# First stage of a decoder layer: the weights of modulation tile 0 in quarters and their sums shared out anew between TensorE and VectorE, the first hT tile in two PSUM banks, one norm weight loaded later

## The chip, the core and the metric

The kernel runs on one core of a Trainium2 chip. A core has a tensor engine (PE; its weight loads have a row of their own, PEld), a vector engine (DVE), a scalar engine (ACT), a further engine for general work (POOL), and a queue for loads and stores (SP); ACT and POOL can issue loads too. Each engine works through its own list in order, and waits where an instruction needs what another engine or a load has not delivered. PE writes its results to PSUM banks of 128 partitions by 512 values in float32. The metric is the device time of one execution in microseconds (us), the median of a few runs; lower is better.

## What is computed

One layer of a decoder with two token mixers beside each other and a gated MLP, float32, sequence 512, width 1024. The change touches what stands at the beginning:

```python
cs = jax.nn.silu(c)                                   # c: (1, 1024)
mod = cs @ w_ada[l] + b_ada[l]                        # six vectors of 1024
shift1, scale1, gate1, shift2, scale2, gate2 = ...
h = _rmsnorm(x, norm1_g[l]) * (1.0 + scale1) + shift1
proj = h @ w_in[l]                                    # columns of the mixers and gates
...
out = _rmsnorm(out, subln_g) * (1.0 - lam_init)       # heads of the second mixer
```

`x` is 512 by 1024, `w_ada` 1024 by 6144. The rest (attention, merging, output projection, MLP with a causal convolution, final norm) is unchanged in both kernels.

## The kernel before

The first stage makes the first 768 columns of `proj` (query, key and value of the first mixer). The width is cut into KT = 8 tiles of 128 features. For tile k the stage needs:

- two vectors of 128, the scale and the shift of the modulation. They are sums over 1024 inputs of `w_ada`, times `cs`. The weights of tile k lie in `adaw[k]`, 128 partitions by (j, kk, 128): j = 0 the scale's half, j = 1 the shift's half, kk = 0 to 7 the blocks of inputs. Each half is 512 KB. Some blocks are summed on PE directly (a matmul of the block with `cs` broadcast, `direct` and `direct0`), the others are added up by DVE (`add_a0`, `ac_ops`) and then summed over partitions by one closing matmul with ones (`reduce_mod`; line 474 for tile 0);
- `mods[k]`, made from these sums by `finish_mod`;
- x normalised and transposed: PE transposes four blocks of 128 rows into a bank `xt` (`turn` for tile 0, line 432; `h_turn` for the others, line 378);
- `hT`, scale and shift applied to `xt`: ACT writes a rounded copy `hTh` and an exact one `hf` (`h_tile`, line 383), DVE the remainder `hTl` (`h_low`, line 391);
- the weights `w0[k]` (128 by 768), split into a rounded part `w0h` (ACT, lines 361 and 363) and a remainder `w0l` (DVE, lines 369 and 371).

Then `mm_k` (line 403) multiplies: six groups i of 128 columns, each in a bank of its own (`acc6`, a0 to a5), and three products p: `w0h` by `hTh`, `w0l` by `hTh`, `w0h` by `hTl`. One product of one group is one matmul of 512 columns. The order of PE, DVE and ACT in this stage is that in which the code is written (`manual_schedule`, line 259); SP's order too (line 243). Later parts are ordered by a scheduler.

At the start x comes in as four blocks of 128 rows. For each, ACT takes the sum of squares (`stat`, line 414), POOL and DVE form the root, and DVE or ACT scale the first 256 columns; the other columns are scaled by ACT later (`scale_x`). `keep_warm` (line 184) issues matmuls with ones into a5 whose result nobody reads; they fill PE until data are there. For tile 0, PE sums blocks 0 to 4 of both halves and DVE blocks 5 to 7. The two sums lie in the banks `pa0` and a4.

From tile 1 on, one turn of the loop (line 482) is, for PE: the products p = 0 and 1 of tile gi, the closing sums of tile gi + 1, its transposes, and product p = 2 of tile gi. DVE adds up the weights of the tile after. In turn 0 the closing sums of tile 1, each behind two direct sums, stand before the two matmuls of group 5.

SP's list is: c (as 8 rows `crow8`, line 166), the four blocks of x, `adaw[0]` in two halves, `w0[0]`, then `adaw[k]` and `w0[k]` by turns (the tiles 1 to 4 in quarters of 256 KB, the others in halves), four small loads (lines 251 to 256), and the weights of the next stage (line 567). ACT issues three small loads at the start: `b_ada`, `norm1_g` and `diff_subln_g`, all into `rows`, which one transpose turns into columns (`cols`, line 272).

Of the kernel before, what the change touches and what calls it, by code (L numbers as in the profile page):

```python
# [14 lines left out]
P = 128  # L15
D = 1024
# [44 lines left out]
def kernel(  # L61
# [44 lines left out]
    def tbank(name, shape=(P, S)):  # L106
        return bank("t", 2, list(shape), name)
# [55 lines left out]


    crow8 = cpool.tile([8, P], F32, name="crow8")
    nc.sync.dma_start(crow8, c.rearrange("o (a p) -> (o a) p", p=P))
# [13 lines left out]
    def keep_warm(n):  # L180
        while n:
            m = min(n, 4)
            o = acc6[5].rearrange("p (a n) -> p a n", a=4)
            nc.tensor.matmul(o[:, :m], ones, ones4[:, :m], start=True, stop=True)
            n -= m
# [38 lines left out]
    def load_ada(k):  # L224
        if k % 3 == 2:
            aw = big.tile([P, 2, KT, P], F32, tag="out" + "hl"[k // 3], name=f"adaw{k}")
        else:
            aw = pp.tile([P, 2, KT, P], F32, tag="adaw", bufs=2, name=f"adaw{k}")
        cut = 4 if 0 < k < 5 else KT
        for a in range(0, KT, cut):  # L230
            for j, base in ((0, D), (1, 0)):
                nc.sync.dma_start(
                    aw[:, j, a : a + cut],
                    wada[a * P : (a + cut) * P, base + k * P : base + (k + 1) * P].rearrange("(a p) n -> p a n", p=P),
                )
        adaw[k] = aw
# [6 lines left out]
    with tc.manual_schedule(engines={nc.sync.engine}):  # L243
        for t in range(NT):
            nc.sync.dma_start(xn[:, t], xd[t * P : (t + 1) * P, :])
# [10 lines left out]
        nc.sync.dma_start(crow[66:88, :], conv_b[0].rearrange("(a p) -> a p", p=P))  # L256
# [15 lines left out]
    nc.tensor.transpose(pc, rows, ident[:NR, :NR])  # L272
    cols = cpool.tile([P, NR], F32, name="cols")
    nc.vector.tensor_copy(cols, pc)
    bsh, bsc1, n1g, sublnc = cols[:, 0:8], cols[:, 8:16], cols[:, 16:24], cols[:, 24:25]
# [28 lines left out]
    def direct(pa, j, k, kks, start=True, stop=False):  # L304
        for kk in kks:
            nc.tensor.matmul(
                pa[:, j],
                adaw[k][:, j, kk],
                cs[:, kk : kk + 1].to_broadcast([P, P]),
                start=start and kk == kks[0],  # L310
                stop=stop and kk == kks[-1],
            )

    def early_mod(gi):
        pa = tbank(f"pa{gi}", (P, 2, P))
        direct(pa, 0, gi, (6, 7))
        return pa

    def reduce_mod(gi, early=None):
        pa = early or tbank(f"pa{gi}", (P, 2, P))  # L320
        for j in range(2):
            if early:
                if j:
                    direct(pa, 1, gi, (6, 7))
                nc.tensor.matmul(pa[:, j], ac[gi][0][:, j], ones, start=False, stop=True)
            else:
                nc.tensor.matmul(pa[:, j, 0:1], ac[gi][0][:, j], ones[:, 0:1], start=True, stop=True)
        return pa

    def finish_mod(k, pa):  # L330
        pa = pa if k == 0 else [pa[:, 0], pa[:, 1]]
        m = pp.tile([P, 16], F32, tag="mod", bufs=3, name=f"mod{k}")
        last = nc.vector.scalar_tensor_tensor(
            m[:, 0:1], pa[0][:, 0:1], bsc1[:, k : k + 1], n1g[:, k : k + 1], ALU.add, ALU.mult
        )
        if k:
            nc.scalar.activation(m[:, 1:2], pa[1][:, 0:1], AF.Identity, bias=bsh[:, k : k + 1])
        else:
            nc.vector.tensor_add(m[:, 1:2], pa[1][:, 0:1], bsh[:, k : k + 1])
        mods[k] = m  # L340
        return last

    def w0_views(k):
# [29 lines left out]
    hfs, pts = {}, {}  # L373

    def h_turn(k):
        pts[k] = tbank(f"xt{k}")
        for t in range(NT):
            nc.tensor.transpose(pts[k][:, t * P : (t + 1) * P], xn[:, t, k * P : (k + 1) * P], ident)

    def h_tile(k, between=None):  # L380
        hf = pp.tile([P, S], F32, tag="hf", bufs=2, name=f"hf{k}")
        for dst in (hTh[k], hf):
            nc.scalar.activation(dst, pts[k], AF.Identity, bias=mods[k][:, 1:2], scale=mods[k][:, 0:1])
# [11 lines left out]
    def mm_k(k, part, some=DONE):  # L395
        wh, wl = wts[k]
        last = k == KT - 1
        if part == (2 if last else 1):
            return
        for i in some:  # L400
            for p in (1, 2) if last and part else (0, 1) if part == 0 and not last else (part,):
                lhs, rhs = ((wh, hTh), (wl, hTh), (wh, hTl))[p]
                nc.tensor.matmul(
                    acc6[i], lhs[:, i * P : (i + 1) * P], rhs[k], start=k == 0 and p == 0, stop=last and p == 2
                )

    keep_warm(WARM)
    rst = pp.tile([P, NT], F32, name="rst")
# [17 lines left out]
    def scale_head(t):  # L426
        nc.scalar.activation(xn[:, t, :HEAD], xn[:, t, :HEAD], AF.Copy, scale=rst[:, t : t + 1])

    pts[0] = tbank("xt0")

    def turn(t):
        nc.tensor.transpose(pts[0][:, t * P : (t + 1) * P], xn[:, t, 0:P], ident)
# [6 lines left out]
    DIRECT = 5  # L439

    def add_a0(j, kks):
        for kk in kks:
            w, f = adaw[0][:, j, kk], cs[:, kk : kk + 1]
            if kk == DIRECT:
                nc.vector.tensor_scalar_mul(a0[j], w, f)
            else:
                nc.vector.scalar_tensor_tensor(a0[j], w, f, a0[j], ALU.mult, ALU.add)

    def direct0(j):
        for kk in range(DIRECT):  # L450
            nc.tensor.matmul(
                pa0[j], adaw[0][:, j, kk], cs[:, kk : kk + 1].to_broadcast([P, P]), start=kk == 0, stop=False
            )
# [12 lines left out]
    scale_x(0)  # L466
    scale_head(2)
    scale_head(3)
    scale_x(1)
    direct0(0)  # L470
    turn(2)
    direct0(1)
    for j in range(2):
        nc.tensor.matmul(pa0[j], a0[j], ones, start=False, stop=True)
    turn(3)
    finish_mod(0, pa0)
    split_hi(0, 0)
    keep_warm(2)
    h_tile(0, lambda: split_hi(0, 1))
    split_lo(0, 0)  # L480

    for gi in range(KT):
# [8 lines left out]
        else:  # L491
# [64 lines left out]
        nc.scalar.copy(va, pv.rearrange("p (t d) -> p t d", t=NT))  # L556


    pcv = tbank("pcv", (P, 88))
    nc.tensor.transpose(pcv, crow, ident[:88, :88])  # L560
# [1499 lines left out]
```

## Time and profile before

| | |
|---|---|
| median of 3 runs | 685.23 us (684.86 to 685.31) |
| span of the profiled execution, first to last instruction | 684.1 us |
| busy: PE, PEld, DVE, ACT, POOL | 675.3, 589.7, 564.2, 384.5, 98.5 us |
| first matmul of the projection | at 15.36 us |
| first matmul of the next stage | at 55.59 us |
| DMA in the slices of 17.1 us from the start | 304, 349, 296, 181 GB/s |

The profile is one execution. A row of its timeline gives the start and the duration in us, the engine, the line of the kernel, the operation, its output and inputs, and how many instructions are merged in the row; in brackets stands how long the engine had been idle before and what ended that. Names are those of the program without buffer numbers: `a` is any of the banks a0 to a5 (or DVE's sums of tile 0), `w` stands for `w0`. A float32 matmul appears as two passes, a weight load and a matmul each. The windows give busy times of each engine in stretches of the span; the waits say who waited for whom.

### The profile page before, as it was taken

How to read it: one execution, taken by the hardware profiler on the slowest of the kernel's cores; microseconds unless marked ns; L12 is line 12 of the kernel's file. 1: busy time of each engine (PE TensorE's matmuls, PEld its weight loads, DVE VectorE, ACT ScalarE, POOL GpSimd, SP SyncE). 2: the span in 40 equal slices, each digit the busy share in tenths (PEclk: the TensorE clock that was granted, in tenths of full speed). 3: DMA queues.
4: the chain of work that ended last, by engine and by line, in shares of the span. 5: the costliest groups of instructions: out<-in, count | busy, mean ns of one | idle time of the engine just before them, and what ended most of it. 6: DMA issues, size and time to landing. Idle time of an engine off the chain costs nothing. (4 is left out here: it accounts for less than half of the span.)

```text
span 684.1 us, 11125 instructions
## 1 busy us (share of the span) xinstructions
PE 675.3 (99%) x4141; PEld 589.7 (86%) x4141; DVE 564.2 (82%) x1075; ACT 384.5 (56%) x688; POOL 98.5 (14%) x119
## 2 busy tenths in 40 slices
PE   9999999999999999999999999999999999999995
PEld 5887887878888888888899999999999998888885
DVE  4999875988796756974589988888888999979997
ACT  6776774546543223324377665666555665656765
POOL 3000000011012012021030111112120003440300
PEclk9999999999999999999999999999999999999999
DMA  9995422565456885659555788777978647995903
GB/s 304 349 296 181 144 62 64 163 166 162 144 157 181 255 246 158 217 144 345 187 93 109 170 216 212 180 165 207 216 194 216 153 170 186 191 205 146 166 1 123
DMA packets 117142, 123.89 MB, mean 181 GB/s; under 512 B 5063, under 2 KB 94184, under 8 KB 117088
## 3 DMA queue, kind: packets, MB, share of 16 engines
q1 hardware_dynamic: 97246, 95.11, 43.3%
q0 software_dynamic: 19648, 27.79, 24.1%
q8 instruction: 32, 0.52, 0.3%
q10 hardware_dynamic: 194, 0.28, 0.1%
q14 instruction: 22, 0.18, 0.1%
HBM read 118.97 MB, written 2.11 MB: 177 GB/s over the span
## 5 line engine op out<-in xcount | busy, mean ns | idle before, releaser
L1362 PE MATMUL up<-t,m_whi 128*128 128x256 f32 x512 | 93.1, 283 | 0.0
L1362 PEld LDWEIGHTS up<-t,m_whi 128*128 128x128 f32 x512 | 79.9, 192 | 0.0
L1362 PE MATMUL up<-t,m_wlo 128*128 128x256 f32 x256 | 72.4, 283 | 0.0
L1362 PE MATMUL up<-bh,p_whi 128*128 128x256 f32 x232 | 65.7, 283 | 0.0
L1362 PE MATMUL up<-bl,p_whi 128*128 128x256 f32 x232 | 65.7, 283 | 0.0
L1362 PE MATMUL up<-bh,p_wlo 128*128 128x256 f32 x232 | 65.7, 283 | 0.0
L952 POOL DMA_DIRECT2D arow<-arow x28 | 22.5, 804 | 247.8 <-DVE sd L821 123.6
L1362 PEld LDWEIGHTS up<-t,m_wlo 128*128 128x128 f32 x256 | 49.2, 192 | 0.0
L1271 POOL DMA_DIRECT2D s<-in_w_up_dram x21 | 26.9, 1353 | 141.3 <-DMA s<-in_w_up_dram 69.2
L1362 PEld LDWEIGHTS up<-bh,p_whi 128*128 128x128 f32 x232 | 44.5, 192 | 0.0
L1362 PEld LDWEIGHTS up<-bl,p_whi 128*128 128x128 f32 x232 | 44.5, 192 | 0.0
L1362 PEld LDWEIGHTS up<-bh,p_wlo 128*128 128x128 f32 x232 | 44.5, 192 | 0.0
L944 DVE SCALAR_TENSOR_TENSOR arow<-ra,cs,arow 128x512 f32<-128x512 f32 x56 | 41.8, 748 | 0.6
L1299 ACT CAST m_whi<-s 128x1024 fp32r<-128x1024 f32 x31 | 32.4, 1046 | 11.1 <-DVE s L1293 6.3
L1303 DVE TENSOR_TENSOR m_wlo<-s,m_whi 128x1024 fp32r<-128x1024 f32 x31 | 37.8, 1218 | 0.0
L1362 PE MATMUL up<-t,p_whi 128*128 128x256 f32 x176 | 32.2, 283 | 0.0
L1362 PEld LDWEIGHTS up<-t,p_whi 128*128 128x128 f32 x176 | 27.5, 192 | 0.0
L816 ACT ACTIVATE sd<-sd,dmx 128x128 f32<-128x128 f32 (+3 forms) x32 | 17.7, 557 | 17.3 <-DVE dmx L806 17.3
L1369 ACT ACTIVATE gT<-a,cv 128x512 f32<-128x512 f32 x22 | 17.7, 813 | 16.9 <-DVE a L1404 15.8
L1299 ACT CAST p_whi<-wa 128x1024 fp32r<-128x1024 f32 x18 | 18.7, 1041 | 12.6 <-PE up L1362 12.6
L1303 DVE TENSOR_TENSOR p_wlo<-wa,p_whi 128x1024 fp32r<-128x1024 f32 x18 | 22.0, 1222 | 3.8 <-ACT p_whi L1299 3.8
L1362 PE MATMUL up<-t,p_wlo 128*128 128x256 f32 x88 | 24.9, 283 | 0.0
(499 smaller groups left out, 2052.4 us busy)
## 6 DMA issues: line engine op xcount, KB each, us to landing
ra<-in_w_ada_dram SPq DMA_DIRECT2D x32, 512.0 KB, 4.9
wa<-in_w_up_dram SPq DMA_DIRECT2D x22, 512.0 KB, 4.2
s<-in_w_up_dram SPq DMA_DIRECT2D x21, 512.0 KB, 4.7
s<-in_w_up_dram POOLq DMA_DIRECT2D x21, 512.0 KB, 6.9
w<-in_w_in_dram SPq DMA_DIRECT2D x12, 512.0 KB, 5.0
a<-in_w_up_dram SPq DMA_DIRECT2D x11, 512.0 KB, 4.7
b<-in_w_down_dram SPq DMA_DIRECT2D x10, 512.0 KB, 4.2
adaw<-in_w_ada_dram SPq DMA_DIRECT2D x8, 512.0 KB, 6.3
```

The costliest lines, as they stand in the source:

```text
L816: exp = nc.scalar.activation(pm[m], pm[m], AF.Exp, bias=mx[:, m : m + 1], scale=slope, accum_out=ls)
L944: nc.vector.scalar_tensor_tensor(ac, r[:, a], cc, ac, ALU.mult, ALU.add)
L952: nc.gpsimd.dma_start(whole[0:n], whole[n : 2 * n], accum_op=ALU.add)
L1271: nc.gpsimd.dma_start(dst, upblock(*blk), accum_op=ALU.add)
L1299: nc.scalar.copy(W[J, name][0], R[J, SRC[name]])
L1303: nc.vector.tensor_sub(lo, R[J, SRC[name]], hi.bitcast(F32))
L1362: nc.tensor.matmul(o[u], w[:, k, cu], b[:, k], start=name in ("p1", "m5", "p2") and k == 0 and x == 0, stop=k == 3 and x == 2, skip_group_ ...
L1369: nc.scalar.activation(grow(j), av[J][:, u], AF.Identity, bias=cv[:, 66 + j : 67 + j], scale=cv[:, 44 + j : 45 + j])
```

## The change

Five edits, all but one of them to the first stage.

1. The load of c moves from SP's queue to ACT's, ahead of ACT's other two. `diff_subln_g` leaves `rows`; it is loaded by SP behind the convolution's bias into a row more of `crow`, and its column comes out of the later transpose of `crow` (`cv`).
2. `adaw[0]` is loaded in quarters, the two of the scale first.
3. The sums of tile 0 are shared out anew. Scale: blocks 0 to 5 on PE, 6 and 7 on DVE. Shift: blocks 0 and 1 on DVE, 2 to 7 on PE. Blocks are summed in the order in which they come, between the turns of x. The scale's part of `mods[0]` (`mod_scale`) is followed by the shift's. Two fillers go, and tile 1's transposes stand before `h_tile(0)`.
4. `xt` of tile 0 lies in two banks: rows 0 to 255 in a bank of its own, rows 256 to 511 in a5. `h_tile(0)` makes the first half of `hTh` on DVE and the second on ACT; `hf` in two pieces on ACT.
5. `mm_k` of tile 0 does all `w0h` products before the `w0l` products. Tile 1's four direct sums come together, then the two matmuls of group 5, then the two closing sums. The large part of tile 1's `w0l` is split behind `finish_mod`, as in the other turns.

```diff
-    nc.sync.dma_start(crow8, c.rearrange("o (a p) -> (o a) p", p=P))
-    NR = 16 + 8 + 1
+    nc.scalar.dma_start(crow8, c.rearrange("o (a p) -> (o a) p", p=P))
+    NR = 16 + 8
...
-    nc.scalar.dma_start(rows[24:25, :], diff_subln_g)
-    crow = cpool.tile([88, P], F32, name="crow")
+    crow = cpool.tile([89, P], F32, name="crow")
...
-        cut = 4 if 0 < k < 5 else KT
-        for a in range(0, KT, cut):
-            for j, base in ((0, D), (1, 0)):
+        cut = 4 if k < 5 else KT
+        pieces = [(a, j) for a in range(0, KT, cut) for j in range(2)]
+        if k == 0:
+            pieces.sort(key=lambda e: e[1])
+        for a, j in pieces:
+            for base in ((D, 0)[j],):
...
         nc.sync.dma_start(crow[66:88, :], conv_b[0].rearrange("(a p) -> a p", p=P))
+        nc.sync.dma_start(crow[88:89, :], diff_subln_g)
...
-    nc.vector.tensor_scalar_mul(sublnc, sublnc, -0.5 * (1.0 - LAM_INIT))
...
     def early_mod(gi):
         pa = tbank(f"pa{gi}", (P, 2, P))
-        direct(pa, 0, gi, (6, 7))
+        for j in range(2):
+            direct(pa, j, gi, (6, 7), start=j == 0)
         return pa
...
             if early:
-                if j:
-                    direct(pa, 1, gi, (6, 7))
-                nc.tensor.matmul(pa[:, j], ac[gi][0][:, j], ones, start=False, stop=True)
+                nc.tensor.matmul(pa[:, j], ac[gi][0][:, j], ones, start=False, stop=True, skip_group_check=True)
...
         for dst in (hTh[k], hf):
-            nc.scalar.activation(dst, pts[k], AF.Identity, bias=mods[k][:, 1:2], scale=mods[k][:, 0:1])
+            for src in pts[k]:
+                q = slice(src[1], src[1] + src[0].shape[-1])
+                if k == 0 and dst is not hf and src[1] == 0:
+                    nc.vector.tensor_scalar(dst[:, q], src[0], mods[k][:, 0:1], mods[k][:, 1:2], ALU.mult, ALU.add)
+                else:
+                    nc.scalar.activation(
+                        dst[:, q], src[0], AF.Identity, bias=mods[k][:, 1:2], scale=mods[k][:, 0:1]
+                    )
...
+        order = [(i, p) for i in some for p in ps_]
+        if k == 0:
+            order.sort(key=lambda e: e[1])
...
-    pts[0] = tbank("xt0")
+    HALF = S // 2
+    pts[0] = [(tbank("xt0", (P, HALF)), 0), (acc6[5][:, :HALF], HALF)]
...
-            keep_warm((4, 1)[t - 1])
+            if t == 1:
+                keep_warm(4)
+                direct0(0, range(4), True)
     root(2)
-    add_a0(0, range(DIRECT, DIRECT + 2))
+    add_a0(0, (6,), 6)
     root(3)
-    add_a0(0, range(DIRECT + 2, KT))
-    add_a0(1, range(DIRECT, KT))
+    add_a0(0, (7,), 6)
+    add_a0(1, (0, 1), 0)
     scale_x(0)
     scale_head(2)
     scale_head(3)
     scale_x(1)
-    direct0(0)
+    direct0(0, (4, 5))
+    direct0(1, (2, 3), True)
     turn(2)
-    direct0(1)
-    for j in range(2):
-        nc.tensor.matmul(pa0[j], a0[j], ones, start=False, stop=True)
+    sum0(0)
     turn(3)
-    finish_mod(0, pa0)
+    direct0(1, range(4, KT))
+    sum0(1)
+    mod_scale(0, pa0[0][:, 0:1])
+    nc.vector.tensor_add(mods[0][:, 1:2], pa0[1][:, 0:1], bsh[:, 0:1])
     split_hi(0, 0)
-    keep_warm(2)
+    h_turn(1)
     h_tile(0, lambda: split_hi(0, 1))
     split_lo(0, 0)
...
-        if gi == 0:
-            h_turn(1)
         mm_k(gi, 0, DONE if gi else FIRST[:5])
         mm_k(gi, 1)
         if more:
+            early = None
             if gi == 0:
-                split_lo(1, 0)
-            pa = reduce_mod(gi + 1, early_mod(1) if gi == 0 else None)
-            if gi == 0:
+                early = early_mod(1)
                 mm_k(0, 0, FIRST[5:])
+            pa = reduce_mod(gi + 1, early)
...
             last_mod = finish_mod(gi + 1, pa)
-            if gi:
-                split_lo(gi + 1, 0)
+            split_lo(gi + 1, 0)
             split_lo(gi + 1, 1)
             h_tile(gi + 1)
...
-    nc.vector.tensor_copy(cv[:, :88], pcv)
+    nc.vector.tensor_copy(cv[:, :89], pcv)
+    sublnc = cv[:, 88:89]
+    nc.vector.tensor_scalar_mul(sublnc, sublnc, -0.5 * (1.0 - LAM_INIT))
```

The names in the rows below carry the program's numbers: `xt0` and `xt1` are the transposed tiles 0 and 1, `pa0` and `a4` the banks of tile 0's scale and shift, `a5` the bank of group 5 (and of the fillers), `a0_0` and `a0_1` DVE's sums of tile 0, `pa1` the bank of tile 1's sums. First PE's list at the start, behind the filler that follows turn 0, in the kernel before:

```order
L432 MATMUL xt0_205<-ident_69,xn_123 128x128
L184 MATMUL a5_113<-ones_67 128x128
L451 MATMUL pa0_206<-cs_188,adaw0_130 128x128 x5
L432 MATMUL xt0_205<-ident_69,xn_123 128x128
L451 MATMUL a4_111<-cs_188,adaw0_130 128x128 x5
L474 MATMUL pa0_206<-ones_67,a0_0_207 128x128
L474 MATMUL a4_111<-ones_67,a0_1_208 128x128
L432 MATMUL xt0_205<-ident_69,xn_123 128x128
L184 MATMUL a5_113<-ones_67 128x256
L378 MATMUL xt1_307<-ident_69,xn_123 128x128 x4
```

And the same place in the changed kernel:

```order
L460 MATMUL pa0_207<-cs_190,adaw0_129 128x128 x4
L442 MATMUL xt0_206<-ident_69,xn_122 128x128
L460 MATMUL pa0_207<-cs_190,adaw0_129 128x128 x2
L460 MATMUL a4_110<-cs_190,adaw0_129 128x128 x2
L442 MATMUL a5_112<-ident_69,xn_122 128x128
L466 MATMUL pa0_207<-ones_67,a0_0_208 128x128
L442 MATMUL a5_112<-ident_69,xn_122 128x128
L460 MATMUL a4_110<-cs_190,adaw0_129 128x128 x4
L466 MATMUL a4_110<-ones_67,a0_1_209 128x128
L377 MATMUL xt1_285<-ident_69,xn_122 128x128 x4
```

Ten direct sums have become twelve; four of them now stand behind the last turn instead of five, and the scale's closing sum has moved ahead of it. Next PE's list at the end of tile 0's `w0l` products, up to the first product with `hTl`, before:

```order
L403 MATMUL a4_111<-hThA_116,w0l0_283 128x512
L306 MATMUL pa1_323<-cs_188,adaw1_135 128x128 x2
L325 MATMUL pa1_323<-ones_67,ac1_0_289 128x128
L306 MATMUL pa1_323<-cs_188,adaw1_135 128x128 x2
L325 MATMUL pa1_323<-ones_67,ac1_0_289 128x128
L403 MATMUL a5_113<-hThA_116,w0h0_282 128x512
L403 MATMUL a5_113<-hThA_116,w0l0_283 128x512
L403 MATMUL a0_110<-hTlA_118,w0h0_282 128x512
```

And in the changed kernel:

```order
L412 MATMUL a4_110<-hThA_115,w0l0_283 128x512
L308 MATMUL pa1_323<-cs_190,adaw1_136 128x128 x4
L412 MATMUL a5_112<-hThA_115,w0h0_282 128x512
L412 MATMUL a5_112<-hThA_115,w0l0_283 128x512
L327 MATMUL pa1_323<-ones_67,ac1_0_294 128x128 x2
L412 MATMUL a0_109<-hTlA_117,w0h0_282 128x512
```

Both closing sums of tile 1 (`ac1`) now stand behind the two matmuls into a5. Last DVE's list at the same time: the end of tile 1's sums (`ac`), its `mod`, the split of its `w0l`, and the start of tile 2's sums, before:

```order
L301 TENSOR_TENSOR ac_0_289<-ac_0_289,ac_1_298 128x256
L391 TENSOR_TENSOR hTlA<-hf_286,hThA 128x512
L369 TENSOR_TENSOR w0l_295<-w_1_140,w0h_294 128x512
L333 SCALAR_TENSOR_TENSOR mod_332<-pa_323,cols 128x1
L371 TENSOR_TENSOR w0l_295<-w_1_140,w0h_294 128x256
L286 TENSOR_SCALAR ac_1_352<-adaw_142,cs 128x256
```

And in the changed kernel:

```order
L303 TENSOR_TENSOR ac_0_294<-ac_0_294,ac_1_304 128x256
L397 TENSOR_TENSOR hTlA<-hf_290,hThA 128x512
L334 SCALAR_TENSOR_TENSOR mod_332<-pa_323,cols 128x1
L367 TENSOR_TENSOR w0l_301<-w_1_141,w0h_300 128x512
L369 TENSOR_TENSOR w0l_301<-w_1_141,w0h_300 128x256
L288 TENSOR_SCALAR ac_1_353<-adaw_143,cs 128x256
```

The large split of tile 1's `w0l` has moved from ahead of the `mod` to behind it, between the `mod` and tile 2's sums.

More of the change, by code (lines that the diff above doesn't have):

```diff
@@ L328, in reduce_mod, with mod_scale @@
         return pa
+    def mod_scale(k, pa):
+        m = mods[k] = pp.tile([P, 16], F32, tag="mod", bufs=3, name=f"mod{k}")
+        return nc.vector.scalar_tensor_tensor(m[:, 0:1], pa, bsc1[:, k : k + 1], n1g[:, k : k + 1], ALU.add, ALU.mult)
     def finish_mod(k, pa):
[L331 to L340, printed above, removed]
+        last = mod_scale(k, pa[:, 0, 0:1])
+        nc.scalar.activation(mods[k][:, 1:2], pa[:, 1, 0:1], AF.Identity, bias=bsh[:, k : k + 1])
         return last
@@ L375, in h_turn @@
     def h_turn(k):
-        pts[k] = tbank(f"xt{k}")
+        xt = tbank(f"xt{k}")
+        pts[k] = [(xt, 0)]
         for t in range(NT):
-            nc.tensor.transpose(pts[k][:, t * P : (t + 1) * P], xn[:, t, k * P : (k + 1) * P], ident)
+            nc.tensor.transpose(xt[:, t * P : (t + 1) * P], xn[:, t, k * P : (k + 1) * P], ident)
     def h_tile(k, between=None):
@@ L399, in mm_k @@
             return
[L400 to L405, printed above, removed]
+        ps_ = (1, 2) if last and part else (0, 1) if part == 0 and not last else (part,)
+        order = [(i, p) for i in some for p in ps_]
+        if k == 0:
+            order.sort(key=lambda e: e[1])
+        for i, p in order:
+            lhs, rhs = ((wh, hTh), (wl, hTh), (wh, hTl))[p]
+            nc.tensor.matmul(
+                acc6[i], lhs[:, i * P : (i + 1) * P], rhs[k], start=k == 0 and p == 0, stop=last and p == 2
+            )
     keep_warm(WARM)
@@ L427, in scale_head @@
         nc.scalar.activation(xn[:, t, :HEAD], xn[:, t, :HEAD], AF.Copy, scale=rst[:, t : t + 1])
-    pts[0] = tbank("xt0")
+    HALF = S // 2
+    pts[0] = [(tbank("xt0", (P, HALF)), 0), (acc6[5][:, :HALF], HALF)]
     def turn(t):
-        nc.tensor.transpose(pts[0][:, t * P : (t + 1) * P], xn[:, t, 0:P], ident)
+        nc.tensor.transpose(pts[0][t // 2][0][:, t % 2 * P : (t % 2 + 1) * P], xn[:, t, 0:P], ident)
     def scale_x(t):
@@ L447, in add_a0, with direct0, sum0 @@
                 nc.vector.scalar_tensor_tensor(a0[j], w, f, a0[j], ALU.mult, ALU.add)
-    def direct0(j):
-        for kk in range(DIRECT):
+    def direct0(j, kks, start=False):
+        for kk in kks:
             nc.tensor.matmul(
-                pa0[j], adaw[0][:, j, kk], cs[:, kk : kk + 1].to_broadcast([P, P]), start=kk == 0, stop=False
-            )
+                pa0[j], adaw[0][:, j, kk], cs[:, kk : kk + 1].to_broadcast([P, P]), start=start and kk == kks[0],
+                stop=False,
+            )
+    def sum0(j):
+        nc.tensor.matmul(pa0[j], a0[j], ones, start=False, stop=True)
     for t in range(NT):
@@ L556, in turn_va @@
         nc.scalar.copy(va, pv.rearrange("p (t d) -> p t d", t=NT))
-    pcv = tbank("pcv", (P, 88))
-    nc.tensor.transpose(pcv, crow, ident[:88, :88])
+    pcv = tbank("pcv", (P, 89))
+    nc.tensor.transpose(pcv, crow, ident[:89, :89])
     cv = cpool.tile([P, P], F32, name="cv")
-    nc.vector.tensor_copy(cv[:, :88], pcv)
+    nc.vector.tensor_copy(cv[:, :89], pcv)
+    sublnc = cv[:, 88:89]
+    nc.vector.tensor_scalar_mul(sublnc, sublnc, -0.5 * (1.0 - LAM_INIT))
     def load_cols(src, col, name):
```

8 lines of the change are left out of this document (4 added, 4 removed).

## The prediction

> **What bounds the kernel now.** I read the page first (busy time per engine), then the busy time by stretches, then the timeline of the first 56 us, where every edit lies.
>
> ```profile
> span 684.1 us, 11125 instructions
> 100.00:200.00 100.00, 100.00 (x578) 80.29 (x577) 80.63 (x231) 53.66 (x129) 10.73 (x12) 1.00 0.46 132
> ```
>
> The first row is the page's span. The second is one stretch of the windows (us, then busy time and count of PE, PE's weight loads, DVE, ACT and POOL): from 100 to 200 us PE is busy for all 100.00 us, with DVE at 80.63. So PE sets the end, and an edit before 56 us is worth what it moves PE's last wait there, no more. The three timed runs (684.86 to 685.31, median 685.23) lie 0.8 to 1.2 us above this span; I carry that part over unchanged and make the sum against the span.
>
> **The start, up to the first matmul of the projection.** The columns are start, duration, engine, line, output and inputs, count, and in brackets the idle time before.
>
> ```profile
> 9.28 0.34 PE L432 MATMUL xt<-ident,xn 128*128 128x128 f32 x1
> 9.45 1.02 PE L184 MATMUL a<-ones 128*128 128x512 f32 x2
> 10.31 0.29 PE L432 MATMUL xt<-ident,xn 128*128 128x128 f32 x1
> 12.41 1.19 PEld L451 LDWEIGHTS a<-cs,adaw 128*128 128x128 f32 x10 [0.31 <-DMA adaw<-in_w_ada_dram]
> 13.52 0.30 PEld L474 LDWEIGHTS pa<-ones,a 128*128 128x128 f32 x2
> 13.85 0.39 PE L474 MATMUL a<-ones,a 128*128 128x128 f32 x2
> 14.28 0.16 DVE L339 TENSOR_TENSOR mod<-a,cols 128x1 f32<-128x1 f32 x1
> 14.53 0.78 ACT L383 ACTIVATE hThA<-xt,mod 128x512 fp32r<-128x512 f32 x1 [0.59 <-DVE mod L339]
> 15.36 0.50 PE L403 MATMUL a<-hThA,w0h 128*128 128x512 f32 x1
> 15.70 0.39 PE L403 MATMUL a<-hThA,w0l 128*128 128x512 f32 x1
> ```
>
> Ten weight loads of the direct sums fill 12.41 to 13.52, 0.111 us a pass. They wait for the shift half of tile 0's weights (0.31 us, DMA). The last sum's two passes start at 13.85; DVE adds at 14.28 (0.43 later), ACT starts the first hT at 14.53 (0.25 later), and PE's first projection matmul starts at 15.36, 0.05 after ACT's 0.78 us.
>
> In the new order PE's list from 9.28 is: turn 0; one filler of two 512-column passes, 9.45 to 10.31; four direct sums (8 passes, to 11.20), turn 1 (11.31), two direct sums of the scale (11.75), two of the shift (12.20), turn 2 (12.31), the scale's closing sum (12.53), turn 3 (12.64), four direct sums of the shift (13.53), its closing sum at 13.53. That is 0.32 earlier than 13.85. Do its inputs come in time?
>
> ```profile
> 11.90 0.35 DVE L447 SCALAR_TENSOR_TENSOR a<-adaw,cs,a 128x128 f32<-128x128 f32 x1
> 12.08 0.51 ACT L427 ACTIVATE xn<-xn,rst 128x256 f32<-128x256 f32 x1 [0.31 <-DVE rst L205]
> 8.37 0.35 DVE L424 TENSOR_SCALAR xn<-xn,rst 128x256 f32<-128x256 f32 x1
> 11.27 0.49 ACT L427 ACTIVATE xn<-xn,rst 128x256 f32<-128x256 f32 x1
> ```
>
> DVE's last piece of the scale ends at 12.25 and ACT's scaling for turn 3 at 12.59, both before they are needed; the shift's last quarter is needed at 12.64 and landed by 12.41. So PE's own list binds here, and data that come sooner don't help. DVE adds at 13.96, ACT starts at 14.21. ACT now does 256 columns: not under 0.49 (the last row, 256 columns from SBUF) nor over 0.78; I take 0.55, near the row of its size. DVE's half (0.35 in the third row, 256 columns from SBUF; at most 0.78) starts at 14.15 and is covered by ACT's half unless it takes over 0.6. First matmul at 14.8 instead of 15.36: **0.55 us gained** (0.3 to 0.6). The low half of the weights, which DVE makes after its hT half (at about 14.5 to 15.2), is wanted only after five high matmuls (at about 15.9), so that delay is hidden by the new order of tile 0.
>
> **Tile 1: the gain is spent.** The next rows are the sum of tile 1, the DVE work around it, and the same points of tiles 2 and 3.
>
> ```profile
> 18.34 0.69 DVE L369 TENSOR_TENSOR w0l<-w,w0h 128x512 fp32r<-128x512 f32 x1
> 18.88 0.39 PE L325 MATMUL pa<-ones,ac 128*128 128x128 f32 x2
> 19.30 0.22 DVE L333 SCALAR_TENSOR_TENSOR mod<-pa,cols 128x1 f32<-128x1 f32 x1 [0.28 <-PE pa L325]
> 19.44 0.41 DVE L371 TENSOR_TENSOR w0l<-w,w0h 128x256 fp32r<-128x256 f32 x1
> 19.77 0.35 DVE L286 TENSOR_SCALAR ac<-adaw,cs 128x256 f32<-128x256 f32 x1
> 19.85 0.78 ACT L383 ACTIVATE hThA<-xt,mod 128x512 fp32r<-128x512 f32 x1
> 20.94 0.40 PE L403 MATMUL a<-hThA,w0h 128*128 128x512 f32 x1
> 22.90 0.42 DVE L301 TENSOR_TENSOR ac<-ac,ac 128x256 f32<-128x256 f32 x1
> 23.73 0.50 PE L327 MATMUL pa<-ones,ac 128*128 128x1 f32 x4
> 24.09 0.63 PE L378 MATMUL xt<-ident,xn 128*128 128x128 f32 x4
> 28.68 0.61 PE L327 MATMUL pa<-ones,ac 128*128 128x1 f32 x4
> 29.15 0.63 PE L378 MATMUL xt<-ident,xn 128*128 128x128 f32 x4
> ```
>
> Before, tile 1's closing sums (18.88 the last) stood ahead of the two matmuls into a5. Now they stand behind them: two matmuls at 0.23 each (20.94 to 23.73 holds twelve: 0.2325) and about 0.08 for the return from 128 to 512 columns (an estimate; 15.36 to 15.70 shows 0.11 over 0.23 after a wait), so 0.54 later in PE's list. 0.55 earlier and 0.54 later: DVE's mod of tile 1 stays at **19.3**, and ACT's hT of tile 1 at 19.85 to 20.63. PE's next matmul can start at 20.68, 0.26 before 20.94; PE itself would be there at about 20.5.
>
> DVE is the next bound. Its split of w0l1 (18.34, 0.69 us) lay before the mod, in time when DVE had nothing to do. It now stands behind the mod, and everything after it moves by its length less the overlap of two DVE rows (0.08): **0.61**. The first sum of tile 2 moves from 19.77 to 20.38 and its closing add (22.90, 0.42) to 23.51, ending at 23.93. PE's closing sum of tile 2 reads it: it started at 23.73 and can now start at 23.99. So PE, 0.26 ahead at 20.7, waits and is **0.26 behind** at 24.0. Behind that sum queue tile 2's transposes and the six low matmuls of tile 1.
>
> A sum that had to wait also costs more: 28.68 to 29.15 (tile 3, released by DVE) took 0.47, against 0.36 from 23.73 to 24.09. So 0.37 behind after tile 2. At tile 3 PE is then late enough not to wait for DVE, and the old 0.11 falls away: 0.26 behind from there on.
>
> **Tile 7: the lateness is hidden, and the loads decide.**
>
> ```profile
> 0.74 0.40 SPq L166 DMA_DIRECT2D crow<-in_c_dram  x1
> 1.20 1.78 SPq L245 DMA_DIRECT2D xn<-in_x_dram  x4
> 41.06 0.35 SPq L256 DMA_DIRECT2D crow<-in_conv_b_dram  x1
> 41.46 3.62 SPq L567 DMA_DIRECT2D w<-in_w_in_dram  x3
> 49.20 1.05 ACT L128 CAST w_h<-w 128x1024 fp32r<-128x1024 f32 x1 [0.57 <-DMA w<-in_w_in_dram]
> 50.15 0.25 ACT L337 ACTIVATE mod<-pa,cols 128x1 f32<-128x1 f32 x1
> 51.27 1.67 PE L403 MATMUL a<-hThB,w0h 128*128 128x512 f32 x6 [0.19 <-ACT hThB L383]
> ```
>
> Before tile 7's matmuls PE waited 0.19 us for ACT's hT, and after a wait the second matmul comes 0.34 after the first (15.36 to 15.70) instead of 0.23: some 0.30 in all, which takes in the 0.26. ACT was late because its second cast of the next weights (49.20) waited 0.57 for DMA, and mod 7 (50.15) queues behind it. So PE starts tile 7 at 51.27, moved by what moves that load, whatever happened earlier. Two edits do. The load of c leaves SP, so the x loads are issued at 0.74 instead of 1.20: the stream is 0.46 earlier, if that reaches this far. The norm weight's load joins SP's queue just ahead of 41.46: by the row before, 0.35 to 0.42 with the gap, I take 0.40, and the load behind it is issued that much later. Net: **0.06 earlier**.
>
> The rest I cost at nothing. The norm weight's scaling on DVE, one column of 128 rows, moves to about 57 us, where DVE next waits 1.0 us for PE (first row below, from the waits); without that cover it would cost PE its own length, under 0.25. On ACT's queue the load of c takes the first of three places, so the rows of b_ada and norm1_g are issued one place, 0.5 us, later, still 3 us and more ahead of the transpose that reads them (second row); if they came late, the wait would stand there, ahead of the fillers. The fillers that go stood in PE's waits.
>
> ```profile
> DVE st L667 <- PE sw L139: 1.0, 1, 1.0
> 5.48 0.30 PE L272 MATMUL pc<-ident,rows 25*128 25x25 f32 x1
> ```
>
> Sum: 684.1 - 0.06, about 684.0 for the span, and 685.2 for the median.
>
> [...] The quartered load gives four landings instead of two.
>
> ```profile
> 8.00:12.00 4.00, 3.97 (x18) 2.06 (x17) 2.77 (x16) 3.53 (x6) 1.89 (x3) 1.00 1.09 351
> 12.00:15.40 3.40, 3.19 (x26) 2.62 (x24) 2.54 (x9) 2.73 (x5) 0.00 (x0) 1.00 1.12 353
> 4.73 1.06 ACT L414 ACTIVATE sq<-xn 128x1024 f32<-128x1024 f32 x1 [1.40 <-DMA xn<-in_x_dram]
> ```
>
> The last two columns of the windows are the DMA engines' share and GB/s. From 8 to 12 us pieces of 512 KB move (x and tile 0's halves), at 351; from 12 to 15.4 come tile 1's pieces of 256 KB, at 353. So pieces in a row overlap and a further one costs no time. [...]
>
> **Rivals.**
> 1. *The gain is kept.* If DVE closes tile 2 in time (its rows shorter, or mod 1 sooner), PE stays ahead to tile 7, where the load still holds it to the 0.46 of the earlier stream, and only if SP's extra issue costs nothing there. For it: the loads keep their order behind x. Against: DVE's list from mod 1 to the closing add, 3.6 us from 19.30 to 22.90, gets 0.61 longer, and the small issue is there. 683.6, so 684.7.
> 2. *The small load costs more than the early start brings.* Slower, by one place: SP at 41.46. If the stream's 0.46 is lost on the way (x waits for DMA, not for issue), the extra 0.40 remains, ACT casts at 49.60 and PE starts tile 7 at 51.67: 684.5, so 685.6. It decides once less than 0.40 of the 0.46 arrives.
> 3. *The pieces add up.* Slower by more. The first x tile lands 3.5 us after its issue (1.20 to 4.73), of which 512 KB at 351 GB/s are 1.5: 2.0 fixed. If the two added pieces paid that one after the other, the last quarter would land at 16.4, against 12.64 where PE wants it: PE's list moves by 3.8, the first matmul to 18.6, and 3.2 us are lost: 688.5. It decides once a piece lands over 0.2 later than now. Against it: the two windows.
>
> **How the numbers follow.** No change, within about 0.2 of the median: 0.60. The gain kept: 0.18. The small load: 0.12. The pieces add up: 0.02. Something that these rows don't show (another wait after 56 us): 0.04 for each side. A measurement of this kernel can tell about 0.2% from no change, 1.4 us; the first three cases all lie within it, so same has 0.90, slower 0.06 (third rival and unforeseen), faster 0.04. The range takes in rivals 1 and 2 with the runs' own spread of 0.45: 684.3 to 686.1.
>
> **What would show it.** First projection matmul at 14.7 to 15.0; mod 1 within 0.15 of 19.3; PE waiting for DVE's closing add at tile 2's sum, that sum at 23.9 to 24.1; ACT's second cast before tile 7 still waiting for DMA, starting at 48.8 to 49.6. Wrong would be: no wait at tile 2's sum (rival 1), the first x square still at 4.7 and tile 7 at 51.7 (rival 2), PE waiting for DMA in its direct sums (rival 3), or spans that differ after 56 us.

## The result, and the profile after

The changed kernel takes 688.95 us (median of 6 runs, 688.30 to 693.11) against 685.26 for the kernel before in the same series: 3.7 us more, ratio 1.0062 (95% interval 1.0047 to 1.0076). The forecast was no change, with 686.1 as the upper end. The profiled run took 688.6 us; its page:

```profile
span 686.8 us, 11127 instructions
...
PE 675.0 (98%) x4141; PEld 589.5 (86%) x4141; DVE 563.0 (82%) x1074; ACT 384.1 (56%) x689; POOL 98.2 (14%) x119
```

PE is busy as long as before (675.3), so the 2.7 us more of the span are waits. First, the waits of PE in the first 60 us (waiting instruction, what ended the wait, us in total, times, longest), then the timeline at the start and at the places that the prediction named:

```profile
PE pc L275 <- DMA rows<-in_norm_g_dram: 1.9, 1, 1.9
...
PE a L412 <- ACT hThA L387: 0.5, 1, 0.5
PE pa L329 <- DVE ac L303: 0.3, 1, 0.3
```

```profile
1.43 0.33 ACTq L169 DMA_DIRECT2D rows<-in_b_ada_dram  x1
...
1.79 0.34 ACTq L170 DMA_DIRECT2D rows<-in_norm_g_dram  x1
...
7.80 0.27 PE L275 MATMUL pc<-ident,rows 24*128 24x24 f32 x1 [1.91 <-DMA rows<-in_norm_g_dram]
...
8.00 3.60 PE L183 MATMUL a<-ones 128*128 128x512 f32 x4
8.11 0.18 DVE L277 COPY cols<-pc 128x24 f32<-128x24 f32 x1 [3.63 <-PE pc L275]
...
11.44 0.27 PE L442 MATMUL xt<-ident,xn 128*128 128x128 f32 x1
...
15.64 0.39 PE L466 MATMUL a<-ones,a 128*128 128x128 f32 x2
...
16.25 0.56 ACT L387 ACTIVATE hThA<-a,mod 128x256 fp32r<-128x256 f32 x1 [2.15 <-DVE mod L493]
...
16.95 1.38 PE L412 MATMUL a<-hThA,w0h 128*128 128x512 f32 x5 [0.48 <-ACT hThA L387]
...
21.30 0.22 DVE L334 SCALAR_TENSOR_TENSOR mod<-pa,cols 128x1 f32<-128x1 f32 x1 [0.53 <-PE pa L327]
...
22.67 0.50 PE L412 MATMUL a<-hThA,w0h 128*128 128x512 f32 x1
...
25.49 0.42 DVE L303 TENSOR_TENSOR ac<-ac,ac 128x256 f32<-128x256 f32 x1
...
26.06 0.58 PE L329 MATMUL pa<-ones,ac 128*128 128x1 f32 x4 [0.32 <-DVE ac L303]
```

The loads of b_ada and norm1_g (the two ACTq rows) are issued 0.69 and 0.55 us later than before, where they stood so:

```profile
0.74 0.40 ACTq L169 DMA_DIRECT2D rows<-in_b_ada_dram  x1
...
1.24 0.53 ACTq L170 DMA_DIRECT2D rows<-in_norm_g_dram  x1
```

They are waited for much longer: the transpose of these rows, at 5.48 before, stands at 7.80 after 1.91 us of waiting for norm1_g. DVE's copy of the result (8.11) stands ahead of all its work on x, and PE's slow fillers (8.00, 3.60 us for four passes) stand ahead of turn 0, which moves from 9.28 to 11.44.

| | before | predicted | after |
|---|---|---|---|
| turn 0 on PE | 9.28 | 9.28 | 11.44 |
| first projection matmul | 15.36 | 14.8 | 16.95 |
| mod 1 | 19.30 | 19.3 | 21.30 |
| tile 2's closing sums | 23.73 | 23.99 | 26.06 |

From turn 0 to the first projection matmul PE needed 5.51 us against 5.52 predicted and 6.08 before: the gain of the new sharing is there, and starts 2.16 us late. The wait at tile 2's sum is there too (0.32, for DVE's closing add).

The second thing in this trace is spread over the whole stage. The windows from 12 to 24 us (last two columns: share of the DMA engines, GB/s), before and after:

```profile
12.00:24.00 12.00, 11.79 (x71) 9.94 (x70) 10.62 (x27) 10.07 (x19) 0.00 (x0) 1.00 1.12 362
```

```profile
12.00:24.00 12.00, 11.49 (x73) 9.73 (x72) 8.33 (x23) 8.17 (x16) 0.00 (x0) 1.00 1.17 313
```

The DMA engines are as busy as before (1.17 against 1.12) and move 313 GB/s instead of 362. In the landings of the trace, the 256 KB pieces of the modulation weights come 0.90 us apart, before 0.75, and the last piece of the stage (w0[7]) lands at 46.3 instead of 43.7. Nothing in the prediction asks for that.

Last, PE waits 0.38 us at 334 us, in the output projection, where it did not before. Set against the kernel before matmul by matmul, PE is 2.0 us late ahead of this place and 2.75 late after it:

```profile
334.33 0.50 PE L1435 MATMUL oc<-wo_wlo,mg3h 128*128 128x512 f32 x1 [0.38 <-DVE wo_wlo L129]
```

### The profile page after: what moved, and what is told of

The parts are those of the page before. It is cut to its first block, busy times and chain, and to the rows that moved or that the text cites. A ratio compares the mean times of both kernels' runs of the same rounds, so it can differ in the third digit from the quotient of the medians.

```text
span 686.8 us, 11127 instructions
## 1 busy us (share of the span) xinstructions
PE 675.0 (98%) x4141; PEld 589.5 (86%) x4141; DVE 563.0 (82%) x1074; ACT 384.1 (56%) x689; POOL 98.2 (14%) x119
```

## The experiments

Each kernel was timed beside runs of the kernel before on the same chip. GB/s are those of the window from 12 to 24 us; "offset" is where the buffers behind `cols` start, in bytes above a multiple of 256.

| kernel | offset | c issued by | GB/s | first projection matmul | time, us (runs from, to) | before beside it | ratio (95% interval) |
|---|---|---|---|---|---|---|---|
| before | 0 | SP | 362 | 15.36 | | | |
| after | 224 | ACT | 313 | 16.95 | 688.95 (688.30, 693.11) | 685.26 | 1.0062 (1.0047 to 1.0076) |
| c_back | 224 | SP | 314 | 14.89 | 689.69 (688.06, 692.69) | 685.34 | 1.0063 (1.0046 to 1.0081) |
| c_only | 0 | ACT | 360 | 16.90 | 686.65 (686.11, 687.50) | 685.34 | 1.0019 (1.0010 to 1.0028) |
| c_pool | 224 | POOL | 312 | 17.03 | 689.08 (688.76, 690.29) | 685.34 | 1.0057 (1.0044 to 1.0070) |
| late_only | 0 | SP | 361 | 16.16 | 689.05 (687.36, 691.03) | 685.34 | 1.0053 (1.0036 to 1.0071) |
| aligned | 0 | ACT | 334 | 15.81 | 687.22 (686.50, 688.87) | 685.52 | 1.0025 (1.0016 to 1.0034) |
| aligned_c_back | 0 | SP | 363 | 14.69 | 685.48 (685.15, 685.67) | 685.52 | 0.9998 (0.9990 to 1.0007) |
| aligned_c_split | 0 | SP | 362 | 14.78 | 684.94 (684.69, 685.96) | 685.52 | 0.9993 (0.9984 to 1.0002) |
| before_shifted | 224 | SP | 316 | 15.78 | 690.09 (688.61, 693.74) | 685.52 | 1.0069 (1.0048 to 1.0090) |
| off32 | 32 | SP | 314 | 16.04 | 688.75 (687.90, 688.93) | 685.66 | 1.0041 (1.0026 to 1.0055) |
| off64 | 64 | SP | 315 | 15.52 | 689.77 (687.98, 693.04) | 685.66 | 1.0064 (1.0038 to 1.0090) |
| off128 | 128 | SP | 316 | 15.65 | 688.83 (688.23, 689.70) | 685.66 | 1.0049 (1.0034 to 1.0064) |
| off256 | 0 | SP | 362 | 15.54 | 685.51 (684.92, 686.75) | 685.66 | 0.9997 (0.9988 to 1.0007) |

### First: is it the place of c's load?

**c_back**, the changed kernel with one line undone:

```diff
-    nc.scalar.dma_start(crow8, c.rearrange("o (a p) -> (o a) p", p=P))
+    nc.sync.dma_start(crow8, c.rearrange("o (a p) -> (o a) p", p=P))
```

> The changed kernel with one edit undone: the load of c is back on SP, ahead of x. Theory (late rows): in the changed kernel b_ada and norm1_g, behind c on ACT's queue, land behind blocks of x (norm1_g at 7.7 us), PE's transpose of them waits 1.9 us to 7.80, and the fillers behind it put turn 0 at 11.44 instead of 9.28. With c back on SP the transpose is at 5.2 to 5.7, turn 0 at 9.0 to 9.5, the first projection matmul at 14.7 to 15.1, PE still waits for DVE's closing add at tile 2, and the time is 684.8 to 685.8, that of the kernel before. Rival (the new sharing itself costs): quarters, the closing sums behind group 5 or DVE's longer list cost what was lost; first projection matmul later than 15.4, or 1 us and more lost between it and tile 3; time above 686.5.

The start answers as the theory of the late rows has it (transpose at 5.33, first projection matmul at 14.89), and the time does not: 689.69, no better than the changed kernel. What was gained by 15 us is lost to loads. The timeline between 36 and 39 us, where the longest wait of PE stands:

```profile
36.55 0.91 ACT L290 ACTIVATE ac<-adaw,cs 128x256 f32<-128x256 f32 x2 [2.61 <-DMA adaw<-in_w_ada_dram]
...
37.36 0.24 ACT L338 ACTIVATE mod<-pa,cols 128x1 f32<-128x1 f32 x1
...
38.47 0.50 PE L412 MATMUL a<-hThA,w0h 128*128 128x512 f32 x1 [1.42 <-ACT hThA L387]
```

ACT waits 2.61 us for a piece of the modulation weights, mod queues behind it on ACT, hT behind mod, and PE stands still for 1.42 us. So a second cause is at work, and it is in the loads.

**c_only**, the kernel before with that line alone changed the other way.

> The kernel before with one edit alone: the load of c on ACT's queue ahead of its other three. Late rows: the transpose of the rows waits until 7 to 8.5 us (its third load lands last), turn 0 at 11.0 to 12.0, the first projection matmul at 17.0 to 18.0; at tile 7 some 0.3 is hidden by the wait that was there; 686.5 to 688.5. Rival (the new sharing itself costs): this edit alone leaves 684.8 to 685.8.

Here ACT issues three loads behind c; the transpose waits 1.38 us for the last of them (6.91). First projection matmul at 16.90, 1.54 late; the time is 1.3 us longer. The wait that PE had at tile 7 goes, as expected, and takes back 0.45 of it (on what that wait was, see tile 7 below). The loads run at 360 GB/s, as in the kernel before.

**c_pool**, c on POOL's queue ahead of `ones`:

```diff
+    crow8 = cpool.tile([8, P], F32, name="crow8")
+    nc.gpsimd.dma_start(crow8, c.rearrange("o (a p) -> (o a) p", p=P))
     ones = cpool.tile([P, P], F32, name="ones")
```

> The changed kernel with the load of c on POOL's queue, ahead of everything POOL does: x keeps its early start at 0.74, b_ada and norm1_g are first on ACT's queue again. Late rows: transpose of the rows at 5.2 to 5.9, turn 0 at 9.0 to 9.7, first projection matmul at 14.6 to 15.3; 684.3 to 685.8. If it is x starting early that holds the small loads back, and not their place behind c, they still land after 5 us and turn 0 is after 10.5: 686 to 688. Rival (the new sharing itself costs): above 686.5 with turn 0 at 9.0 to 9.7.

Neither. The rows, first on ACT's queue again, land at 3.7 and 4.6, but now c itself, issued at 1.28 when two blocks of x were on their way, is late: PE waits 2.20 us for it, until 6.13, and the transpose of the rows queues behind that (8.73). Over the traces of c_back, c_only, c_pool, late_only (next), the kernel before and the changed one, the landing of a small load (0.5 to 8 KB) goes by the blocks of x (512 KB each) issued ahead of it, whichever queue it is in: it lands at 2.1 to 3.7 us behind none or one, at 4.1 to 6.3 behind two, at 6.7 to 7.7 behind three or four.

**late_only**, ten filler units more ahead of x (`WARM = 18` for 8) in the kernel before.

> The kernel before with ten more filler units (128 columns each) on PE ahead of the blocks of x and nothing else: a start that is late by itself. Turn 0 at about 11.4 and the first projection matmul at about 17.5, as late as in the changed kernel or a little later. If lateness alone makes the wait of 0.38 us at 334 us and the wide spread of runs (688.3 to 693.1): 687.5 to 690 and a spread above 1 us. If those come from another edit or from the loads: 686.8 to 687.4 (2.15 later, less 0.3 hidden at tile 7), spread below 0.7.

This was not the clean test that it was meant to be. Most of the added fillers ran at the fast rate (0.43 us a pass from about 8.0 us on), so that the start was only 0.80 late (16.16), and the longer program moved one cast of the next stage's weights (ACT) from behind tile 6's mod to ahead of it. There it waits for its load, and PE with it:

```profile
45.74 1.06 ACT L128 CAST w_h<-w 128x1024 fp32r<-128x1024 f32 x1 [1.97 <-DMA w<-in_w_in_dram]
...
47.82 0.50 PE L403 MATMUL a<-hThB,w0h 128*128 128x512 f32 x1 [0.81 <-ACT hThB L383]
```

So its 689.05 says nothing on lateness alone; c_only, whose engines keep their order but for the moved issue, has to serve for that. Its profiled run is its fastest (687.36); what makes the others slower was not seen, though its buffers stand at offset 0 and its loads run at 361 GB/s.

What else separates the kernels at 312 to 314 GB/s from those at 360 to 362 is a size (beside the other edits, which c_back and c_pool share with the changed kernel): `cols` has 24 columns in the first group and 25 in the second, because the norm weight left `rows`. 25 columns are 100 bytes of a partition and take 128 in the built kernels, 24 columns take 96 (`cols` starts at byte 11040 of a partition, the buffer placed next at 11168 or at 11136). All that is placed behind `cols` (x, `adaw`, `w0`, the hT tiles) stands 32 bytes lower: `adaw[0]` starts at byte 169952 of a partition instead of 169984, which is 664 times 256.

### Second: the address alone, and both causes together

**aligned**, the changed kernel with one unused column:

```diff
-    cols = cpool.tile([P, NR], F32, name="cols")
-    nc.vector.tensor_copy(cols, pc)
+    cols = cpool.tile([P, NR + 1], F32, name="cols")
+    nc.vector.tensor_copy(cols[:, :NR], pc)
```

> The changed kernel with one unused column more in cols (25 instead of 24), so that every buffer placed behind it stands at the address that it had before the change, a multiple of 256 bytes, and not 32 bytes lower. Theory (32 bytes off): in the three runs with 24 columns the 256 KB pieces of the modulation weights land 0.90 us apart, in the three with 25 columns 0.74; the address of the buffers does that. Then pieces land 0.74 to 0.77 apart; the late rows stay (transpose of the rows at 7 to 8, first projection matmul at 16.3 to 17.1), some 0.4 of it is hidden at tile 7; 686.2 to 687.4, spread below 1.5. Rival (the quartered load of tile 0, or another edit, slows the stream): 0.88 and more apart, 688 to 690.

**before_shifted**, the kernel before with 224 bytes of padding:

```diff
     cols = cpool.tile([P, NR], F32, name="cols")
+    pad = cpool.tile([P, 56], F32, name="pad")
+    nc.gpsimd.memset(pad[:, :1], 0.0)
```

> The kernel before with 224 bytes of padding behind cols and no other edit, so that the buffers stand 32 bytes below a multiple of 256, as in the changed kernel. 32 bytes off: pieces 0.88 to 0.92 apart from tile 0 on, engines wait for loads between 20 and 50 us, 686.5 to 690 and runs 1 us and more apart. Rival: pieces 0.74 to 0.77 apart and 684.8 to 685.8.

Both came out as the address has it: 0.75 us between pieces in the one, 0.89 in the other. In before_shifted every engine has the order of the kernel before (POOL has one memset more), and it costs 4.6 us. It shows the wait of c_back again, at the same place; ACT's is of the same length, PE's a little shorter (1.16 for 1.42):

```profile
36.65 0.91 ACT L290 ACTIVATE ac<-adaw,cs 128x256 f32<-128x256 f32 x2 [2.61 <-DMA adaw<-in_w_ada_dram]
...
38.57 0.50 PE L405 MATMUL a<-hThA,w0h 128*128 128x512 f32 x1 [1.16 <-ACT hThA L385]
```

In aligned the transpose of the rows still waits (6.77, 0.82 us for norm1_g), less long in the profiled run than expected, with the first projection matmul at 15.81 where 16.3 to 17.1 was expected; 1.7 us are left in the median, and the runs lie 2.4 us apart, not within 1.5. Its 334 GB/s are not a slower rate: the stream paused twice in that window (pieces of 384 KB came 1.76 and 1.40 us after the piece ahead), and the pieces of 256 KB came 0.75 apart; why it paused is open.

**aligned_c_back** has both edits, **aligned_c_split** puts DVE's split of tile 1's w0l ahead of mod 1 besides:

```diff
+                split_lo(1, 0)
             pa = reduce_mod(gi + 1, early)
...
-            split_lo(gi + 1, 0)
+            if gi:
+                split_lo(gi + 1, 0)
             split_lo(gi + 1, 1)
```

> The same, and c back on SP ahead of x: both suspects gone, the rest of the change in place. 32 bytes off and late rows: pieces 0.74 to 0.77 apart, first projection matmul at 14.7 to 15.1, PE waits 0.1 to 0.4 for DVE's closing add at tile 2, that lateness is hidden at tile 7; 684.6 to 685.7, as the prediction has it. Rival: 0.88 and more apart, 688 to 690 as without the column.

> As aligned_c_back, and DVE splits the large part of tile 1's w0l ahead of mod 1, where it stood before the change. If that split is what makes PE wait at tile 2, the wait is below 0.1, and PE is 0.3 to 0.6 ahead of the kernel before from there to tile 7. If tile 7 is held by the load of the next stage's weights, the time is that of aligned_c_back within 0.3; if nothing holds it there, 0.3 to 0.6 less: 684.2 to 685.4 between the two.

With both causes gone the rest of the change is worth nothing, as forecast: 685.48 against 685.52 (why, stands under tile 7 below). This kernel is the place to read the prediction's steps undisturbed:

```profile
9.14 0.27 PE L442 MATMUL xt<-ident,xn 128*128 128x128 f32 x1
...
13.38 0.39 PE L466 MATMUL a<-ones,a 128*128 128x128 f32 x2
...
14.00 0.56 ACT L387 ACTIVATE hThA<-a,mod 128x256 fp32r<-128x256 f32 x1 [0.29 <-DVE mod L493]
14.00 0.54 DVE L385 TENSOR_SCALAR hThA<-xt,mod 128x256 fp32r<-128x256 f32 x1
...
14.69 1.39 PE L412 MATMUL a<-hThA,w0h 128*128 128x512 f32 x5 [0.48 <-ACT hThA L387]
...
19.04 0.22 DVE L334 SCALAR_TENSOR_TENSOR mod<-pa,cols 128x1 f32<-128x1 f32 x1 [0.53 <-PE pa L327]
...
20.43 0.50 PE L412 MATMUL a<-hThA,w0h 128*128 128x512 f32 x1
...
23.24 0.42 DVE L303 TENSOR_TENSOR ac<-ac,ac 128x256 f32<-128x256 f32 x1
...
23.81 0.58 PE L329 MATMUL pa<-ones,ac 128*128 128x1 f32 x4 [0.33 <-DVE ac L303]
```

And with the split moved back, the wait of 0.33 at tile 2 is gone: the sums there start at 23.41, right behind the matmuls.

```profile
23.41 0.50 PE L329 MATMUL pa<-ones,ac 128*128 128x1 f32 x4
```

That kernel is 0.6 us below the kernel before in the median, the best of all; its interval still includes 1.

### Third: which addresses are fast?

The kernel before with other amounts of padding, 32, 64, 128 and 256 bytes.

> The kernel before with 32 bytes of padding behind cols and no other edit: every buffer behind it starts 32 bytes above a multiple of 256 (in before_shifted 32 below it). Multiples of 256 alone are fast: the 256 KB pieces land 0.78 to 0.92 us apart (0.74 in the kernel before) and the time is 686 to 690. Multiples of 64 are enough: slow here too, as above. Rival (only something peculiar to 32 bytes below, as a short first piece, is slow): 0.74 to 0.76 and 685.0 to 685.8.

> The same with 64 bytes. Multiples of 256 alone are fast: 0.78 to 0.92 apart, 686 to 690. Multiples of 64 are enough: 0.74 to 0.76, 685.0 to 685.8.

> The same with 128 bytes. Multiples of 256 alone are fast: 0.78 to 0.92 apart, 686 to 690. Multiples of 64 or 128 are enough: 0.74 to 0.76, 685.0 to 685.8.

> The same with 256 bytes. Multiples of 256 are fast: 0.74 to 0.76 apart, 685.0 to 685.8. If only the addresses of the kernel before are (multiples of 512, the length of a packet of the modulation weights): 0.78 to 0.92, 686 to 690.

Of the four only 256 is fast. The windows from 12 to 24 us of off128 and off256:

```profile
12.00:24.00 12.00, 11.61 (x67) 9.60 (x66) 9.62 (x26) 9.06 (x17) 0.00 (x0) 1.00 1.15 316
```

```profile
12.00:24.00 12.00, 11.46 (x67) 9.66 (x65) 10.35 (x27) 9.90 (x19) 0.00 (x0) 1.00 1.12 362
```

The single packets of 512 bytes in which the modulation weights travel say the same: their median between 12 and 25 us is 27 ns in the kernel before and in off256, and 32 or 33 ns at offsets 32, 64, 128 and 224.

## Why the prediction was wrong

**The step that failed first** is in the part that costed the rest at nothing: "the rows of b_ada and norm1_g are issued one place, 0.5 us, later, still 3 us and more ahead of the transpose that reads them". The issue moved about as much as it said (0.69 and 0.55). But the step measured the margin from the issue, and the transpose waits for the landing. Before, the two were issued at 0.74 and 1.24 and landed at 2.39 and 3.49; after, at 1.43 and 1.79, they landed at 6.17 and 7.67, because the blocks of x, issued early by the same edit, were ahead of them. The trace of before could have warned: ACT's third small load, issued at 1.79 behind two blocks of x, landed at 4.64, 2.85 us later, where the first, issued ahead of x, took 1.65; nothing showed it, since the transpose stood at 5.48. The sentence on what a late landing would cost ("the wait would stand there, ahead of the fillers") held. Price by itself: 1.3 us (c_only), 1.7 (aligned).

**What was missing altogether** is the address. The sum has no term for `rows` and `cols` losing a column; I took it as part of the norm weight's move, which was costed by its instructions and its queue alone. Price by itself: 4.4 us (c_back) and 4.6 (before_shifted) in the medians. The profiled run of each is its fastest, and shows 2.2 and 2.7 us of it in the span; the rest lies in runs without a profile. The forecast had only "something that these rows don't show" for it, with a chance of 0.04, far too small.

The two do not add up: together they cost 3.7 (runs from 688.3 to 693.1). Slow loads hold an early PE back (c_back: 0.81 at tile 2 and 1.42 at 38 us), while a PE that starts 2 us late meets most of the same loads when they have landed; after tile 7 both kernels stand some 2 us behind the kernel before (2.0 and 2.2, matched matmul by matmul). So undoing either one alone shows little: c_back alone would have cleared the late rows of any blame.

**The start, PE's list up to the first projection matmul,** was right: first projection matmul at 14.69 (predicted 14.8) in aligned_c_back, ACT's half 0.56 (0.55), DVE's half 0.54 (0.35 to 0.78).

**Tile 1 and 2** were right in mechanism, 0.2 to 0.3 off in place: mod 1 at 19.04 (19.3, outside the 0.15 I gave), PE's wait at tile 2's sum 0.33 (the sum at 23.81, predicted 23.99, outside 23.9 to 24.1), and aligned_c_split shows that DVE's moved split makes that wait.

**Tile 7** was wrong: in aligned_c_back no load decides there, and no wait hides the lateness. PE is only 0.08 us behind the kernel before ahead of tile 7, not 0.26. ACT casts the next weights without a wait, and PE reaches tile 7 at 51.00, by its own list. off256, whose lists are those of the kernel before, has no wait there either:

```profile
47.09 2.00 ACT L128 CAST w_h<-w 128x1024 fp32r<-128x1024 f32 x2
```

```profile
47.17 2.00 ACT L128 CAST w_h<-w 128x1024 fp32r<-128x1024 f32 x2
```

The first row is from aligned_c_back, the second from off256. So the 0.57 us of waiting for DMA in the profile of before was a property of that execution: its stream paused twice between 24 and 36 us (one piece of 384 KB came 2.06, another 2.45 us after the piece ahead of it, where 0.95 is usual), that of aligned_c_back once (1.71). I took one execution's wait for the kernel's. That aligned_c_back takes as long as the kernel before, as forecast, is in this part luck: the lateness was too small to show, not hidden by a wait.

**The rivals.** That the gain is kept (684.7) needs the split back in its place (684.94) and both causes gone. The small load on SP and the pieces' fixed costs show nowhere: aligned_c_back has the quartered load and the extra SP issue, and 363 GB/s, and tile 0's quarters land 0.74 to 0.78 us apart, as those of the later tiles do. That the third rival's 688.5 lies near the measured 688.95 is chance.

**What stays open.** The runs with shifted buffers scatter over 1.0 to 5.1 us, where those of aligned_c_back lie within 0.5. But late_only, at offset 0, scatters over 3.7, so the address is not the only cause of scatter, and a profile shows one run of each kernel. The wait of 0.38 us at 334 us in the changed kernel comes behind a load that POOL issues 9.6 us later than before (319.3 for 309.7), after a chain of accumulating transfers that lost a little at every step. Two kernels whose edit moves no load have the same wait, off32 and off64, in this order:

```profile
334.49 0.50 PE L1421 MATMUL oc<-wo_wlo,mg3h 128*128 128x512 f32 x1 [0.47 <-DVE wo_wlo L129]
```

```profile
336.57 0.50 PE L1421 MATMUL oc<-wo_wlo,mg3h 128*128 128x512 f32 x1 [1.93 <-DVE wo_wlo L129]
```

They are the kernel before with padding alone, so the moved load of c is not needed for it, and in off64 PE loses 2.2 us there, matched matmul by matmul: a part of what a slow run can lose. No profile at offset 0 has this wait, but neither have c_back, c_pool, before_shifted and off128, which are shifted. What decides between them stays open; the late issue by itself does not, since aligned_c_back issues that load at 319.9 and has no wait.

## What to carry to other kernels

A column, a row or a small tile that goes away can move the buffers placed behind it (here by 32 bytes, one column of `cols`): before costing an edit, look at where the large buffers start before and after, and keep those that loads fill at multiples of 256 bytes (here 360 to 363 GB/s on them and 312 to 316 off them; one unused column put them back). The margin of a load runs from its landing, not its issue: a small load that something waits for early goes ahead of the large ones, on whichever queue (here it landed at 2.1 to 3.7 us behind none or one block of x, at 6.7 to 7.7 behind three or four). And where an edit that is undone changes nothing, undo the other suspect as well before clearing it: two causes that fill the same wait hide each other.

## What the runs showed of the hardware

Loads into buffers that start off a multiple of 256 bytes (32, 64, 128 or 224 above one) ran at 312 to 316 GB/s between 12 and 24 us instead of 360 to 363, with the DMA engines at least as busy (share 1.13 to 1.17 against 1.12); aligned, whose stream paused twice there, is left out. It was the written side of the loads that was shifted. 128 bytes above a multiple is slow (off128, 316 GB/s), the next multiple fast again (off256, 362). How far off the buffers stood made little difference: the packets of 512 bytes took 1.17 to 1.20 times as long at all four offsets (means of 31.5 to 32.5 ns against 27.0). Why they take longer there is not shown.

PE's fillers of 512 columns took 0.85 us a pass until about 9.4 us before and until about 11.3 us after, 0.43 from then on. Where the change of rate falls differs from execution to execution: the four fillers behind the transpose of the rows took 3.78 us in the kernel before and in off128 and 2.56 in before_shifted, with the same lists up to there and no wait for the rows, and in c_back, without that wait too, all four were fast:

```profile
5.51 1.98 PE L183 MATMUL a<-ones 128*128 128x512 f32 x4
```

So a part of the 2.16 us by which turn 0 is late in the profile of the changed kernel may be this rate and not the wait: DVE had scaled the first block of x at 10.10, and PE was busy with slow fillers until 11.4. Whether PE's standing still from 5.9 to 7.8 us made the slow passes last longer is not shown.
